# Moving VectorE's instruction-fetch jump and adding one for SyncE in a load-bound mean kernel

## The chip, the cores and the metric

The kernel runs on one core of one Trainium2 chip. The metric is the device time in microseconds (us). Smaller is better. Times of a few tenths matter here, so single runs are listed as well as medians.

Engine names: VectorE (DVE in the profile), ScalarE (ACT), TensorE (PE), GpSimd (POOL), SyncE (SP). SyncE issues all the transfers of this kernel (every DMA issue of the page stands under SPq).

## The reference

```python
x = np.random.randn(64, 256, 8192).astype(np.float32)   # 16384 rows of 32 KB, 536.87 MB
def reference(x):
    return np.mean(x, axis=2)
```

Nothing is reused: every byte is read once, summed, and 64 KB are written (the page counts 536.87 MB read and 0.07 MB written). The memory stream is the whole problem.

## The kernel before

The rows are read in 63 loads of 8 MB (128 partitions, 2 rows each), into three slots. VectorE sums each. The last 256 rows come as one row per partition and then in chunks of falling size, so that little work is left behind the last byte.

```python
    nc.vector.addr_align(FETCH_BLOCK, offset=0, max_nops=0)     # FETCH_BLOCK = 128
    ...                                                         # identity, memsets
    for n in range(LB):                                         # LB = 63
        xt = slots[n % SLOTS]                                   # SLOTS = 3
        ld = load(xt[:], x_v[n], load_sem[n % LOAD_SEMS])
        if n == 0:
            first = ld
        ...                                                     # VectorE sums xt into res
    ...                                                         # last row set: LAST_CHUNKS =
    ...                                                         #   4096, 2048, 1024, 512, 256, 256
    scaled_sum(fin[0][:, 0:1], head[:])
    store_last(0)
    untracked(scaled_sum(fin[1][:, 0:1], fin_in[:, 0 : lastw + k]))._wait_ge(sem, 16)
    store_last(1)                                               # the last store, by SyncE
    ...
    head_bb, body_bb = nc.main_func.blocks[:2]                  # head_bb ends in a barrier
    body_bb.instructions.remove(first.ins)                      # the first load goes ahead
    at = ...                                                    #   of SyncE's part of it
    head_bb.instructions.insert(at, first.ins)
```

By its name and arguments, `addr_align` asks for the engine's next instruction to stand at a multiple of `FETCH_BLOCK`, which the program calls a fetch block. What the trace of this kernel shows of it is one COMPARE_BRANCH of 47 ns on VectorE at 0.847 us. This document calls it a jump. A packet of 8192 bytes of the kind "instruction" follows at 6.616 us. This document calls it a fetch. Where an engine stands still for some tenths of a microsecond without a jump, and such a packet follows, this document reads it as the engine running on past the end of a block and calls it a "natural crossing".

## Time and profile before

| | before |
|---|---|
| device time, 3 runs | 1247.87 us (1247.67 to 1247.88) |
| span of the profiled run | 1246.0 us |
| read rate over the span | 431 GB/s |
| round (one load of 8 MB) | 19.35 us, of which VectorE sums 17.22 |

Four lines of the profile page of the kernel before: the busy tenths of the DMA engines in 40 slices of the span, then the queues with packets, bytes and share, then the chain that ended last.

```profile
DMA  9999999999999999999999999999999999999998
q1 hardware_dynamic: 10168, 536.94, 99.7%
q14 instruction: 2, 0.02, 0.0%
DMA 70%; DVE 29%; SPq 0%; issue 0%; DVEq 0%
```

The DMA engines are busy throughout (9 tenths or more in 39 of the 40 slices). The third line: two packets of 8192 bytes each, and the one at 6.616 us ran among the packets of load 0.

VectorE's timeline of the kernel before, from the start (start, duration, instruction, and in brackets how long the engine was idle before it and what ended that):

```profile
1.46 0.12 DVE L75 MEMSET fin<- 128x32 f32 x2 [1.46 <-PEq L193]
22.46 17.22 DVE L95 TENSOR_REDUCE res<-xt 128x2 f32<-128x16384 f32 x1 [20.87 <-DMA xt<-in_x_dram]
41.80 17.22 DVE L95 TENSOR_REDUCE res<-xt 128x2 f32<-128x16384 f32 x1 [2.13 <-DMA xt<-in_x_dram]
```

VectorE is ready at 1.5 us and idle for 20.87 us, until load 0 has landed. It then waits about 2.13 us in every round. The first sum starts at 22.456 us, 0.02 us after the last of load 0's sixteen semaphore events (22.433). So a short delay of VectorE's start is taken up by these 20.87 us, and a delay of a landing is taken up by nothing.

The end of the chain of waits of the kernel before (start, duration, what):

```profile
1202.25 38.48 DMA xt<-in_x_dram
1240.73 0.02 issue
1240.76 1.45 DVE fin_in L95 x3
...
1242.34 0.45 DVE fin_in L101 x2
1242.79 0.02 issue
1242.82 0.21 DVE fin_t L112
```

The chain stops at the last VectorE instruction. What follows on SyncE is seen in its own instructions of the closing lines, between 1244.6 and 1245.2 us (count, duration in ns min/median/max, first and last start):

```profile
L169 SPq DRAIN  x2: 7/60/114, 1244.7 to 1245.1; - x2
L169 SPq EVENT_SEMAPHORE  x1: 28/28/28, 1244.6 to 1244.6; - x1
```

The wait at 1244.6 is for the last store. The next wait that the trace lists for SyncE is that of the closing barrier, behind both drains, and yet the two drains stand 0.43 us apart.

### The profile page before, as it was taken

What the parts mean: (1) busy time and instruction counts of PE and PEld (TensorE: products, weight loads), DVE (VectorE), ACT (ScalarE), POOL (GpSimd) and SP (SyncE); (2) the same over time, 40 slices, a digit from 0 to 9 for tenths busy, and PEclk for the clock granted to TensorE, in tenths of its full rate; (3) what the DMA queues carried; (4) which work ended last, traced back from release to release, by engine and by line L of the source; (5) the groups of instructions that cost most, each with busy time, mean ns of one, the idle gap of its engine ahead of it and who ended that gap; (6) DMA issues with size and microseconds to landing.
All of it is one profiled execution on the core that took longest, in us unless ns stands there. A gap on an engine that the chain in (4) does not pass through costs nothing.

```text
span 1246.0 us, 224 instructions
## 1 busy us (share of the span) xinstructions
PE 0.9 (0%) x2; PEld 0.4 (0%) x2; DVE 1087.3 (87%) x79; ACT 16.4 (1%) x13; POOL 0.7 (0%) x6
## 2 busy tenths in 40 slices
PE   0000000000000000000000000000000000000000
PEld 0000000000000000000000000000000000000000
DVE  2898988989889889898898988989889889898897
ACT  0000000000000000000000000000000000000004
POOL 0000000000000000000000000000000000000000
DMA  9999999999999999999999999999999999999998
GB/s 434 425 421 438 438 438 436 438 427 417 438 438 438 438 438 436 429 414 438 438 438 438 438 436 431 412 438 438 438 438 438 436 431 417 433 438 438 438 438 339
DMA packets 10170, 536.96 MB, mean 431 GB/s; under 512 B 1145, under 2 KB 1464, under 8 KB 1720
## 3 DMA queue, kind: packets, MB, share of 16 engines
q1 hardware_dynamic: 10168, 536.94, 99.7%
q14 instruction: 2, 0.02, 0.0%
HBM read 536.87 MB, written 0.07 MB: 431 GB/s over the span
## 4 chain that ended last, share of the span: by engine, by line
DMA 70%; DVE 29%; SPq 0%; issue 0%; DVEq 0%
DMA xt<-in_x_dram 70%; DVE res L95 29%; DVE fin_in L95 0%; SPq L85 0%; DVE fin_in L101 0%; DVE fin_t L112 0%; DVEq L101 0%
## 5 line engine op out<-in xcount | busy, mean ns | idle before, releaser
L95 DVE TENSOR_REDUCE res<-xt 128x2 f32<-128x16384 f32 (+1 forms) x63 | 1076.4, 17086 | 153.1 <-DMA xt<-in_x_dram 153.1
L98 ACT ACT_TABLE_LOAD x1 | 1.3, 1283 | 1181.6 <-DVE res L95 1181.6
L98 ACT ACTIVATE xt<-xt 128x8192 f32<-128x8192 f32 (+5 forms) x6 | 14.7, 2443 | 43.9 <-DMA xt<-in_x_dram 43.7
L95 DVE TENSOR_REDUCE fin_in<-xt 128x1 f32<-128x256 f32 (+3 forms) x5 | 4.9, 1005 | 0.3 <-DMA xt<-in_x_dram 0.2
L95 DVE TENSOR_REDUCE head<-xt 128x1 f32<-128x4096 f32 x1 | 4.4, 4420 | 0.2 <-DMA xt<-in_x_dram 0.2
L156 PE MATMUL ps<-ident,res 128*63 128x128 f32 x2 | 0.9, 460 | 1230.7 <-ACT xt L98 1229.6
L75 DVE MEMSET fin<- 128x32 f32 x2 | 0.1, 85 | 1.5 <-PEq L193 1.5
L98 ACT ACTIVATION_READ_ACCUMULATOR xt<-xt 128x1 f32 x6 | 1.1, 186 | 0.0
L157 DVE TENSOR_SCALAR bulk<-ps 63x128 f32<-63x128 f32 x2 | 0.6, 278 | 0.4 <-PE ps L156 0.4
L156 PEld LDWEIGHTS ps<-ident,res 128*63 128x63 f32 x2 | 0.4, 180 | 1230.9 <-issue 1229.6
L101 DVE TENSOR_SCALAR_CACHE_REDUCE fin_in<-fin_in 128x265 f32<-128x265 f32 x1 | 0.4, 430 | 0.2 <-DVE fin_in L95 0.2
L112 DVE STREAM_TRANSPOSE fin_t<-fin 128x32 f32<-128x32 f32 x2 | 0.4, 212 | 0.1
L63 POOL TENSOR_SCALAR_AFFINE_SELECT ident<-ident 128x128 f32<-128x128 f32 x1 | 0.3, 292 | 0.1
L101 DVE TENSOR_SCALAR_CACHE_REDUCE head<-head 128x2 f32<-128x2 f32 x1 | 0.2, 155 | 0.1
L62 POOL MEMSET ident<- 128x128 f32 x1 | 0.2, 204 | 0.4 <-POOLq L193 0.4
L193 POOL MEMSET const-bfloat16-1.0<- 128x1 bf16 x1 | 0.1, 101 | 0.0
L193 POOL MEMSET const-uint8-127<- 128x1 uint8 x1 | 0.1, 101 | 0.0
L193 POOL MEMSET const-float32-0.0<- 128x1 f32 x1 | 0.1, 98 | 0.2 <-issue 0.2
L193 POOL MEMSET const-float32-1.0<- 128x1 f32 x1 | 0.1, 98 | 0.0
L101 DVE DVE_READ_ACCUMULATOR head<-head 128x1 f32 x1 | 0.1, 83 | 0.0
L101 DVE DVE_READ_ACCUMULATOR fin_in<-fin_in 128x1 f32 x1 | 0.1, 83 | 0.0
## 6 DMA issues: line engine op xcount, KB each, us to landing
xt<-in_x_dram SPq DMA_DIRECT2D x1, 4096.0 KB, 31.1
xt<-in_x_dram SPq DMA_DIRECT2D x1, 2048.0 KB, 35.7
xt<-in_x_dram SPq DMA_DIRECT2D x1, 1024.0 KB, 37.7
xt<-in_x_dram SPq DMA_DIRECT2D x63, 40.8
xt<-in_x_dram SPq DMA_DIRECT2D x1, 512.0 KB, 38.5
xt<-in_x_dram SPq DMA_DIRECT2D x1, 256.0 KB, 38.7
xt<-in_x_dram SPq DMA_DIRECT2D x1, 128.0 KB, 38.5
fin_in<-in_x_dram SPq DMA_DIRECT2D x1, 128.0 KB, 38.4
```

The source lines that it names most:

```text
L62: nc.gpsimd.memset(ident[:], 0.0)
L63: nc.gpsimd.affine_select(out=ident[:], in_=ident[:], compare_op=mybir.AluOpType.not_equal, fill=1.0, base=0, pattern=[[-1, P]], channel_m ...
L75: nc.vector.memset(fin[r][:], 0.0)
L95: return untracked(nc.vector.tensor_reduce(out=dst, in_=src, axis=X, op=ADD))
L98: return untracked(nc.scalar.activation(out=src, in_=src, func=COPY, accum_out=dst))
L101: return nc.vector.tensor_scalar(out=src, in0=src, scalar1=inv, scalar2=None, op0=mybir.AluOpType.mult, op1=ADD, accum_out=dst,)
L112: nc.vector.transpose(out=fin_t[r][:], in_=fin[r][:])
L156: nc.tensor.transpose(out=ps[:LB, :], in_=res[:, r, :], identity=ident[:])
L157: nc.vector.tensor_scalar_mul(out=bulk[:LB, :, r], in0=ps[:LB, :], scalar1=inv)
L193: nc = _bacc.Bacc("TRN2", target_bir_lowering=False, num_devices=1)
```

## The change

The intent is to keep the crossing of fetch blocks off the critical ends. VectorE's jump goes ahead of the head barrier. SyncE gets a jump while VectorE does its last sums, so that it does not cross a block after them.

```diff
-    nc.vector.addr_align(FETCH_BLOCK, offset=0, max_nops=0)
+    jump = nc.vector.addr_align(FETCH_BLOCK, offset=0, max_nops=0)
 ...
-    store_last(0)
+    st = store_last(0)
+
+    with tc.issue_after(st.ins):
+        st = nc.sync.wait_ge(tail_sem[-2], 16)
+    with tc.issue_after(st.ins):
+        st = nc.sync.addr_align(FETCH_BLOCK, offset=0, max_nops=0)
     untracked(scaled_sum(fin[1][:, 0:1], fin_in[:, 0 : lastw + k]))._wait_ge(sem, 16)
-    store_last(1)
+    with tc.issue_after(st.ins):
+        store_last(1)
 ...
-    (first.ins is moved ahead of SyncE's drain in the head)
+    for early in (first.ins, jump.ins):
+        (early is moved ahead of its own engine's drain in the head)
```

The last two entries stand for a short loop, shown in words. The first load was ahead of the barrier already.

More of the change, by code (lines that the diff above doesn't have):

```diff
@@ L112, in store_last @@
         nc.vector.transpose(out=fin_t[r][:], in_=fin[r][:])
-        nc.sync.dma_start(out=out_last[r], in_=fin_t[r][0:P:SQ, :])
+        return nc.sync.dma_start(out=out_last[r], in_=fin_t[r][0:P:SQ, :])
     for n in range(LB):
@@ L170 @@
     head_bb, body_bb = nc.main_func.blocks[:2]
-    assert first.ins in body_bb.instructions
-    body_bb.instructions.remove(first.ins)
-    at = next(
-        i
-        for i, ins in enumerate(head_bb.instructions)
-        if ins.engine == first.ins.engine and isinstance(ins, mybir.InstDrain)
-    )
-    head_bb.instructions.insert(at, first.ins)
+    for early in (first.ins, jump.ins):
+        assert early in body_bb.instructions
+        body_bb.instructions.remove(early)
+        at = next(
+            i
+            for i, ins in enumerate(head_bb.instructions)
+            if ins.engine == early.engine and isinstance(ins, mybir.InstDrain)
+        )
+        head_bb.instructions.insert(at, early)
 _INS = ['x']
```

## The prediction

> What bounds the kernel. The load stream. The page's slices show the DMA engines at least 90% busy in all slices but the last; 536.87 MB are read at 431 GB/s over a span of 1246.0 us. The chain of waits alternates loads (70%) and VectorE sums (29%), but VectorE still waits 2.1 us for a load in each round of 19.35 us, and further loads are always queued. Only the two ends can move.
>
> What the diff really does. SyncE's first load already stood ahead of the head barrier and does not move. VectorE's jump to an aligned fetch block goes ahead of the barrier; SyncE gets a wait for the last chunk but one and then a jump, ahead of its last store.
>
> Head. In the trace VectorE's branch starts at 0.85 us and its next instruction, a memset, at 1.46. That itself costs nothing, as VectorE then waits for load 0 until 22.46. What counts is a side effect. The trace's packet records show one 8192-byte instruction fetch at 6.616 us, 309 ns long, in the middle of load 0 on one DMA engine. That engine's second packet after it starts at 9.866 where the cadence of 2.418 us had it at 9.03: 0.83 us lost. This engine then lands last in load 0 (21.961 against 21.656 for the second last) and still in load 62 (0.311 us behind the second last). A load completes with its slowest engine, so the fetch costs the stream about 0.31 us. I take it to be the fetch that VectorE's jump starts, queued behind two packets. Ahead of the barrier it is asked for near 0.1 us, some 0.75 us earlier; the first load packets start from 1.04 to 1.83 (this engine's at 1.55). If it is served first, all landings come about 0.31 us earlier, and the tail follows. I give that two chances in three; otherwise nothing is gained. The barrier ends perhaps 0.1 us later, so loads 1 and 2 are issued later, which costs nothing.
>
> Tail. After the last store lands, SyncE drains at 1244.678 (7 ns); its next drain starts at 1245.113: 0.43 us, where the step before a drain takes 0.065 us at the head. Another 8192-byte fetch follows at 1245.867. I read this as SyncE running over the end of a fetch block: about 0.36 us on the critical end. [...]the packets here are 8 KiB, and the gap is not hidden. With the change the crossing falls at about 1241.6 to 1242.2, while VectorE works until 1243.03; the last store is not delayed. Gain about 0.36 us, at four chances in five.
>
> Sum: 1247.87 - 0.67 = 1247.2 if both work; weighed, 1247.3 us, range 1246.9 to 1247.8. Faster by over 2%: 0.005; within 2%: 0.99; slower by over 2%: 0.005.
>
> Right if: the early fetch lies before about 1.5 us, the last of load 0's sixteen landings is near 21.65, rounds stay 19.35, SyncE's gap between those drains is about 0.07 us, its branch stands near 1241.6 and the late fetch near 1242.5.
>
> Wrong if: the early fetch still falls among the load's packets, or another engine caused it; the 0.43 us gap is a drain's or branch's own cost and stays; the jump puts code after the kernel onto another block end, outside the span; or runs on a chip differ by more than these tenths.

The sum stands: 1247.87 less 0.67 us (0.31 at the head, 0.36 in the tail) is 1247.2 us if both work. That a load completes with its slowest engine is seen in the trace: the second last of load 0's sixteen semaphore events is at 21.996 us and the last at 22.433, and the first sum starts 0.02 us after the last.

## The result and the profile after

| | before | changed |
|---|---|---|
| device time | 1247.8 us median of 6 (1247.67 to 1248.61) | 1247.2 us median of 6 (1247.08 to 1247.47) |
| span of the profiled run | 1246.0 us | 1245.3 us |

The ratio is 0.9995, with a 95% interval of 0.9982 to 1.0008. A ratio is computed as the mean time of one kernel's runs over that of the other's, so it is not quite the ratio of the medians. This interval is wider than every difference. What is said below of tenths rests on the lists of single runs and on stretches of the traces that repeat from run to run.

VectorE's timeline of the changed kernel at the start:

```profile
1.03 0.13 DVE L75 MEMSET fin<- 128x32 f32 x2 [1.03 <-PEq L200]
22.46 17.22 DVE L95 TENSOR_REDUCE res<-xt 128x2 f32<-128x16384 f32 x1 [21.30 <-DMA xt<-in_x_dram]
41.81 17.22 DVE L95 TENSOR_REDUCE res<-xt 128x2 f32<-128x16384 f32 x1 [2.12 <-DMA xt<-in_x_dram]
```

The memsets come 0.43 us earlier and load 0 not at all: the first sum starts at 22.46 as before. At the start nothing was gained.

The end of the chain of waits of the changed kernel:

```profile
1202.07 38.49 DMA xt<-in_x_dram
1240.56 0.02 issue
1240.59 1.42 DVE fin_in L95 x3
...
1242.15 0.45 DVE fin_in L101 x2
1242.60 0.02 issue
1242.62 0.21 DVE fin_t L112
```

This is 0.2 us earlier than before, although load 0 was not. Comparing the starts of all 63 sums, the kernel before lost 0.11 us in one round (19.46 us in place of 19.35) that the changed kernel did not lose. Experiment 2 comes back to it.

SyncE's drains of the changed kernel between 1244.45 and 1244.65 us, and then the two instructions that the change added:

```profile
L175 SPq DRAIN  x2: 7/10/13, 1244.5 to 1244.6; - x2
```

```profile
L166 SPq NOP  x1: 14/14/14, 1241.6 to 1241.6; - x1
L166 SPq COMPARE_BRANCH  x1: 33/33/33, 1241.6 to 1241.6; - x1
```

The drains stand 0.07 us apart in place of 0.43, and the second takes 7 ns in place of 114. The jump stands at 1241.6 us, while VectorE still works until 1242.83. The trace's record of SyncE's wait for the last store starts only when the store has landed (1244.608 us with its last semaphore event at 1244.591 before, 1244.421 with 1244.405 after). From there to the start of SyncE's last instruction it is 1244.608 to 1245.904 before (1.296 us) and 1244.421 to 1245.240 after (0.819 us), a gain of 0.477 us. It is the gap of 0.37 us plus 0.107 us of the longer drain.

The fetches of the changed kernel lie at 4.195 and 1242.952 us in the trace's packet records (6.616 and 1245.867 before). The DMA view of the changed kernel from 4.18 to 4.52 us shows the first among the packets of the load:

```profile
q1 hardware_dynamic: 9, 0.59, 410.0%
q14 instruction: 1, 0.01, 5.7%
```

So the fetch came earlier but not early enough: the load's packets were already running, the first since 1.041 us.

### The profile page after: what moved, and what is told of

Its sections match the earlier page's. It is cut to its first block, busy times and chain, and to the rows that moved or that the text cites. A ratio compares the mean times of both kernels' runs of the same rounds, so it can differ in the third digit from the quotient of the medians.

```text
span 1245.3 us, 226 instructions
## 1 busy us (share of the span) xinstructions
PE 0.9 (0%) x2; PEld 0.4 (0%) x2; DVE 1087.3 (87%) x79; ACT 16.4 (1%) x13; POOL 0.7 (0%) x6
## 4 chain that ended last, share of the span: by engine, by line
DMA 70%; DVE 29%; SPq 0%; issue 0%; DVEq 0%
DMA xt<-in_x_dram 70%; DVE res L95 29%; DVE fin_in L95 0%; SPq L85 0%; DVE fin_in L101 0%; DVE fin_t L112 0%; DVEq L101 0%
```

## The experiments

After this result there were two theories. Theory A: the whole lasting gain is SyncE's block crossing, about 0.47 us, and VectorE's earlier jump gives nothing because its fetch still falls among load packets. Theory B: VectorE's earlier jump also made the stream 0.15 to 0.2 us shorter, as the earlier chain above suggests.

Kernels 1 to 4 ran on one chip with shared runs of the kernel before (9 runs, 1247.54 to 1247.95, median 1247.73). So did 5 to 8 (1247.65 to 1248.35, median 1247.82) and 9 to 11 (1247.58 to 1248.23, median 1247.83). Each kernel had 5 runs, and all gave correct results. The changed kernel itself ran in the first result and with kernels 1 to 4, where it was 0.6 and 0.48 us below the kernel before. Differences between groups cross chips; for them the distance to the kernel before is given too.

The columns from the third on are of the profiled run: the first fetch after the start, the last of load 0's sixteen landings in the packet records, and the closing stretch on SyncE as above, from the end of its wait for the last store to its last instruction.

| kernel | median (range), us | first fetch | load 0 landed | closing stretch |
|---|---|---|---|---|
| before | see above | 6.616 | 21.961 | 1.296 |
| changed, first run | 1247.2 (1247.08 to 1247.47) | 4.195 | 21.963 | 0.819 |
| 1 changed again | 1247.25 (1247.10 to 1247.49) | 4.178 | 21.943 | 0.819 |
| 2 head move alone | 1247.84 (1247.50 to 1248.31) | 4.556 | 22.320 | 1.297 |
| 3 SyncE's jump alone | 1247.22 (1247.17 to 1247.36) | 6.906 | 22.246 | 0.819 |
| 4 no VectorE jump | 1247.41 (1247.22 to 1248.05) | 838.857 | 21.751 | 0.814 |
| 5 SyncE's jump, no wait | 1247.32 (1247.07 to 1247.46) | 4.281 | 22.053 | 0.813 |
| 6 second VectorE jump | 1248.20 (1248.06 to 1248.38) | 4.393 and 588.147 | 22.158 | 0.819 |
| 7 load behind barrier | 1247.71 (1247.58 to 1247.84) | 1.246 | 22.491 | 0.813 |
| 8 jump behind last store | 1247.17 (1246.97 to 1247.32) | 4.316 | 22.086 | 0.818 |
| 9 VectorE jump first of all | 1247.32 (1247.10 to 1247.54) | 4.423 | 22.185 | 0.820 |
| 10 load behind SyncE's drain | 1247.42 (1247.19 to 1247.51) | 4.186 | 21.952 | 0.813 |
| 11 kernels 8 and 9 together | 1247.45 (1247.12 to 1247.80) | 4.305 | 22.074 | 0.818 |

### 1. The changed kernel again

No edit.

> The changed kernel once more, for the same-chip comparison. Both theories: 0.5 to 0.65 us below the kernel before. Theory A (all of the lasting gain is SyncE's block crossing, 0.36 us of gap plus 0.11 us of drain; the 0.19 us by which the load stream ended earlier in the first profile is scatter of the stream): the span difference averages about 0.47 us. Theory B (VectorE's earlier jump also made the stream 0.15 to 0.2 us shorter): about 0.65 us. The early fetch packet is expected among load 0's packets, near 4.2 us, again.

It was 0.48 us below the kernel before by the medians, and the two lists of runs do not overlap (its slowest is 1247.49, the fastest run of before 1247.54). That is theory A's number.

### 2. The head move alone

```diff
-    with tc.issue_after(st.ins):
-        st = nc.sync.wait_ge(tail_sem[-2], 16)
-    with tc.issue_after(st.ins):
-        st = nc.sync.addr_align(FETCH_BLOCK, offset=0, max_nops=0)
```

> Only VectorE's jump moves; SyncE keeps its natural crossing. Theory A: within 0.1 us of the kernel before; fetch packet near 4.2 us, one engine still 0.84 us behind its cadence, load 0 lands at about 21.96. Theory B: 0.15 to 0.2 us below the kernel before. In both SyncE's gap between its two drains after the last store is 0.43 us again.

It was 0.11 us above the kernel before by the medians, and the lists overlap. Theory B wanted it 0.15 to 0.2 us below. SyncE's two drains of this kernel, between 1245.2 and 1245.75 us:

```profile
L171 SPq DRAIN  x2: 7/60/114, 1245.2 to 1245.7; - x2
```

The gap is back, and so is the drain of 114 ns. The profiled run lost time in two rounds of the stream (19.465 and 19.673 us in place of 19.35), which the kernel before also did, in a different round and by less. Kernels 7, 10 and 11 show such rounds too (up to 19.517, 19.411 and 19.498), and kernels 1, 3, 5, 8 and 9 none above 19.38. So the 0.11 us by which the first profile of before ran late lies inside what the stream scatters. What makes such a round was not found.

### 3. SyncE's jump alone

```diff
-    for early in (first.ins, jump.ins):
+    for early in (first.ins,):
```

> Only SyncE's wait and jump; VectorE's jump stays behind the barrier. Theory A: 0.4 to 0.5 us below the kernel before, equal to the changed kernel within 0.1 us; fetch packet near 6.6 us. Theory B: 0.4 to 0.5 us below before, but 0.15 to 0.2 us above the changed kernel.

It was 0.51 us below before and within 0.03 us of the changed kernel on the same chip, with its fetch at 6.906 us. SyncE's two drains of this kernel, between 1244.7 and 1244.9 us, stand as in the changed kernel:

```profile
L175 SPq DRAIN  x2: 7/10/13, 1244.8 to 1244.8; - x2
```

Together with experiment 2 this settles where the gain came from: SyncE's jump gives all of it, and VectorE's move gives nothing that can be seen.

### 4. No VectorE jump at all

```diff
-    jump = nc.vector.addr_align(FETCH_BLOCK, offset=0, max_nops=0)
-    for early in (first.ins, jump.ins):
+    for early in (first.ins,):
```

> SyncE's jump kept, VectorE's jump taken out[...]. If the 8192-byte fetch near 4.2 us is the one that VectorE's jump starts, it is gone from there, load 0 lands with its second slowest engine at about 21.5 to 21.7 instead of 21.96, and a fetch appears later, 1.3 us or more after a gap of about 0.5 us between two VectorE instructions. If that gap falls in a wait for a load the time is about that of the changed kernel (a late fetch still delays the same engine by 0.8 us); if it falls among the last sums, about 0.5 us is lost there and up to 0.3 us gained from the stream. If another engine causes the fetch, the packet near 4.2 us stays.

The 0.8 us is the estimate from the 0.83 us lost in the trace of before. That a late fetch runs on the same engine is not shown here or in kernel 6, as the packet records carry no engine number.

The fetch among load 0's packets is gone, so it is the one that VectorE's jump starts. Load 0 landed at 21.751 us (21.5 to 21.7 was expected); the eight runs with the early jump, the load at 0 us and a fetch among the packets landed at 22.10 on average (the mean of their rows in the table: changed, 1, 2, 5, 6, 8, 9, 11; from 21.943 to 22.320). The DMA view of this kernel from 0 to 23 us has only one queue left, and the one from 838.8 to 839.2 us shows where the fetch went:

```profile
q1 hardware_dynamic: 160, 9.44, 97.3%
```

```profile
q1 hardware_dynamic: 3, 0.20, 123.7%
q14 instruction: 1, 0.01, 5.2%
```

VectorE's timeline around it:

```profile
834.86 17.22 DVE L94 TENSOR_REDUCE res<-xt 128x2 f32<-128x16384 f32 x1 [2.13 <-DMA xt<-in_x_dram]
854.84 17.22 DVE L94 TENSOR_REDUCE res<-xt 128x2 f32<-128x16384 f32 x1 [2.76 <-DMA xt<-in_x_dram]
```

The fetch ran at 838.857 us, inside the sum that lasts from 834.86 to 852.08. If it followed its crossing, as the fetches of the other traces follow their jumps by 1.02 to 6.1 us, VectorE's natural crossing was over before the wait for the load began at 852.08, and cost VectorE no time that the trace shows. Its fetch does cost: the load in flight lands late, and that round takes 19.98 us in place of 19.35. The gain at the start is paid back in round 42, and the time is that of the changed kernel within the scatter. So the jump at the head does not avoid the cost of the fetch (0.63 us in round 42 here). It moves it.

### 5. SyncE's jump without its wait

```diff
-    with tc.issue_after(st.ins):
-        st = nc.sync.wait_ge(tail_sem[-2], 16)
```

> The changed kernel without SyncE's wait for the last chunk but one: the jump follows the first small store at once, near 1237.6 us, and its 8192-byte fetch is asked for near 1238.9, while the small chunks still come in. If a fetch delays its DMA engine whenever loads are queued on it, the fetch lands among the packets of the chunks and the last landings are 0 to 0.8 us later, by as much as that engine was not ahead of the slowest; the crossing itself is still hidden. Time equal to the changed kernel up to 0.5 us above it. Rival: the fetch costs nothing so late, and the wait is idle care: equal to the changed kernel within 0.1 us.

The jump stood at 1237.725 us and its fetch ran at 1240.935, among the last chunks, 3.2 us after it. The time is within 0.12 us of the changed kernel's (1247.2 and 1247.25 in its two sets) and 0.15 us above kernel 8, with overlapping lists. By the distance to the kernel before (0.50 us, against 0.48 and 0.6 for the changed kernel) it is no slower either. The trace says the same: the last chunk landed 1.315 us after the last chunk but three, against 1.312 in the changed kernel (semaphore events). This does not tell a small cost from none, but no gain from the wait can be seen.

### 6. A second VectorE jump in the middle

```diff
+        if n == 30:
+            with tc.issue_after(prev.ins):
+                prev = nc.vector.addr_align(FETCH_BLOCK, offset=0, max_nops=0)
 ...
```

(`prev` is VectorE's last instruction; each sum is queued behind it, to hold the place of the jump.)

> The changed kernel with one more VectorE jump ahead of sum 30, in a wait of 2.1 us for a load. Theory: the jump of about 0.57 us is hidden in that wait, but it starts one more 8192-byte fetch on the same DMA engine, which is late already, so that engine loses another 0.84 us and every later landing with it: 0.7 to 0.85 us above the changed kernel, one round of about 20.2 us instead of 19.35. Rival: the stream absorbs a single fetch over the remaining rounds: equal to the changed kernel within 0.2 us.

VectorE's timeline around it:

```profile
583.82 17.22 DVE L95 TENSOR_REDUCE res<-xt 128x2 f32<-128x16384 f32 x1 [2.12 <-DMA xt<-in_x_dram]
604.12 17.22 DVE L95 TENSOR_REDUCE res<-xt 128x2 f32<-128x16384 f32 x1 [3.08 <-DMA xt<-in_x_dram]
```

The jump itself:

```profile
L122 DVEq COMPARE_BRANCH  x1: 47/47/47, 583.8 to 583.8; - x1
```

The jump stood at 583.834 us, so it was hidden behind sum 29, which had just started, and not in the wait for load 30 as the expectation had it. That round took 20.30 us in place of 19.35, so one more fetch cost 0.955 us, and the following 32 rounds gave none of it back: every landing after it was late by as much. On the same chip the device time is 0.88 us above kernel 5 (1248.20 against 1247.32) and 0.38 above the kernel before; against the changed kernel on the other chip it is 0.95 (1247.25). Its list of runs overlaps with neither of those two; with that of before it does. The rival falls. The expectation (0.7 to 0.85) was a little low. In the packet records the fetch itself, at 588.147, takes 332 ns, and the packet that starts as it ends takes 3080 ns where 2418 is usual: together 0.99 us on that engine, about the 0.955 that the stream lost.

### 7. The first load behind the barrier

```diff
-    for early in (first.ins, jump.ins):
+    for early in (jump.ins,):
```

> The changed kernel, but the first load goes behind the head barrier, so that VectorE's jump is 0.8 to 0.9 us ahead of it. If what makes the fetch costly is that load packets are queued before it, it is now served first, at about 1.3 to 1.4 us; no packet of load 0 is held for 0.84 us, the slowest engine ends within 0.6 us of the median, and load 0 lands 19.7 to 20.2 us after its first packet, against 20.9 in the changed kernel. The load itself starts some 0.5 to 0.9 us later in the span (SyncE reaches the barrier sooner), so the whole comes out between 0.3 us faster and 0.5 us slower. Rival: the 0.84 us is spent anyway: 0.5 to 0.9 us slower than the changed kernel.

Now the fetch was served first, at 1.246 us, 1.14 us after the jump at 0.102. The DMA view of this kernel from 1.2 to 1.9 us has no packet of a load yet:

```profile
q14 instruction: 1, 0.01, 4.9%
```

Load 0's sixteen landings then lay within 0.53 us, with no single engine left behind; in the changed kernel they spread over 0.97 us with the slowest 0.42 us behind the second slowest. SyncE issued the load 0.95 us later than in the changed kernel, and load 0 landed only 0.39 us later than the average of 22.10. The cost of the fetch is real and can be avoided, but holding the load back costs more than it saves: 1247.71 us, which is only 0.11 us below the kernel before on the same chip, 0.39 above kernel 5 there, and 0.46 above the changed kernel on the other chip. The expected time from first packet to landing was missed (20.51 us measured, 19.7 to 20.2 expected).

### 8. SyncE's jump behind the last store

```diff
-    with tc.issue_after(st.ins):
-        st = nc.sync.wait_ge(tail_sem[-2], 16)
-    with tc.issue_after(st.ins):
-        st = nc.sync.addr_align(FETCH_BLOCK, offset=0, max_nops=0)
     ...
     with tc.issue_after(st.ins):
-        store_last(1)
+        st = store_last(1)
+    with tc.issue_after(st.ins):
+        nc.sync.addr_align(FETCH_BLOCK, offset=0, max_nops=0)
```

> SyncE's jump behind the last store, with no wait before it: the crossing falls between the issue of the store (ends near 1243.37) and its landing (near 1244.2). If only a crossing on the critical end costs, this is as fast as the changed kernel within 0.1 us, with the jump taking about 0.5 us inside that wait and a gap of about 0.07 us between the two drains. If the crossing costs wherever it stands after the last sums, or delays the store's descriptors, it is 0.2 to 0.5 us slower than the changed kernel.

SyncE's jump and then its closing waits and drains in this kernel:

```profile
L167 SPq COMPARE_BRANCH  x1: 33/33/33, 1243.5 to 1243.5; - x1
```

```profile
L173 SPq EVENT_SEMAPHORE  x3: 28/28/28, 1244.0 to 1244.5; - x3
L173 SPq DRAIN  x2: 7/7/7, 1244.6 to 1244.6; - x2
```

After the jump at 1243.514 the next instruction starts at 1243.977, so the jump takes 0.46 us in all. It takes them out of the wait for the store's landing, which SyncE leaves at 1244.514. The closing stretch is 0.818 us and the time 1247.17, 0.65 us below the kernel before of its chip: as good as the changed kernel, with one wait less. So it is not that a crossing is expensive as such (the jump of 0.46 us leaves a closing stretch of 0.818 us here, against 1.296 before): before, it stood a few instructions too late, behind that wait instead of ahead of it.

### 9 to 11. Three tries at getting the fetch ahead of load 0

Kernel 9 puts VectorE's jump ahead of its register set-up:

```diff
-            if ins.engine == early.engine and isinstance(ins, mybir.InstDrain)
+            if ins.engine == early.engine
+            and (early is jump.ins or isinstance(ins, mybir.InstDrain))
```

> The changed kernel with VectorE's jump moved further ahead, to the very first instruction of the program on VectorE, ahead of its register set-up. In the runs so far a fetch follows its jump by 1.15 to 1.3 us and the load packets start at 1.0 to 2.0 us, so the jump at 0.1 us is only just too late. If the jump now stands some tenths of a microsecond before the span's start, its fetch runs before 1.0 us, ahead of load 0: no engine is held for 0.84 us, load 0 lands near 21.75 as without any VectorE jump (21.9 to 22.3 in the runs with the fetch among its packets), and the time is 0.2 to 0.4 us below the changed kernel. Rival: the set-up takes no time, the jump stays near 0.1 us, the fetch stays among the packets and the time is that of the changed kernel.

Kernel 10 lets SyncE's drain go first:

```diff
-        head_bb.instructions.insert(at, early)
+        head_bb.instructions.insert(at + (early is first.ins), early)
```

> The changed kernel with SyncE's first load behind SyncE's own drain, still ahead of the barrier's wait: load 0 is held back by about 0.07 us. If that is enough to let the fetch through on its engine (it missed the engine's first packet by about 0.1 us in the changed kernel's profile, as far as its request can be placed), the fetch appears before 2 us and 0.2 to 0.4 us are gained, less 0.07; if not, the time is that of the changed kernel plus 0 to 0.1 us.

Kernel 11 has kernel 9's edit and kernel 8's.

> VectorE's jump first of all, with SyncE's jump behind the last store in place of the one with the wait: the two variants that promise most, together. If VectorE's early fetch gets ahead of load 0, about 0.3 us below the changed kernel, near 1246.9; if not, equal to it.

The rivals were right in each. In kernels 9 and 11 the jump stayed at 0.094 and 0.093 us, so going ahead of the set-up won no time that the trace shows. In kernel 10 the load began 0.085 us later, which was not enough. In all three the fetch ran after its engine's first packet (4.423, 4.186 and 4.305 us), and none beat the changed kernel: they are 0.51, 0.41 and 0.38 us below the kernel before of their chip. Of all eleven none does clearly; kernel 8 equals it with one wait less.

## Why the prediction was right or wrong

The predicted time was 1247.3 us, with a range of 1246.9 to 1247.8; measured were 1247.2 and, in a second set, 1247.25. That the number fits is in part luck. Weighed by its own odds, the prediction held about 0.21 us for the head (0.31 at two in three) and 0.29 for the tail (0.36 at four in five); the head brought nothing and the tail 0.477, so two errors nearly cancelled.

**The stream bounds the kernel, and only the ends move: right.** Rounds stayed at 19.35 us in every kernel, apart from the slow ones named above.

**"If it is served first, all landings come about 0.31 us earlier": the cost was about right, and it did not happen.** The fetch at 6.616 us is VectorE's (experiment 4: no jump, no fetch there). It costs about what was estimated: load 0 landed 0.35 us earlier without it, in one run against an average of eight that scatter by 0.38. How much of an engine's delay the load feels differs from run to run: in these eight the slowest landing was between 0.05 and 0.89 us behind the second slowest. The 0.955 us of experiment 6 is nearly the whole delay of the engine, as would be so if that engine was already among the last; the records, which carry no engine number, do not show whether it was. The cost comes in two parts. These are the packet records of the engine that ran the fetch, in the kernel before (start and duration in ns), put together by matching ends to starts (to within 4 ns):

```
start    took   what
 4202    2418   64 KB of load 0
 6616     309   8 KB of instructions
 6922    2948   64 KB of load 0
 9866    2418   64 KB of load 0
```

The fetch takes 0.309 us, and the packet after it 0.53 us more than its neighbours (2.948 us against 2.418). In mid-stream it was 0.332 and 0.66 us (kernel 6). The fetch on q14 stands between two packets of q1. Its turn did not come at once: by the estimate below, this fetch was asked for at 1.9 to 2.2 us (the jump at 0.847 plus 1.02 to 1.32), and yet one more packet of the load went ahead of it at 4.202. In kernel 6 too, one more started at 585.732, after the time near 585 at which its fetch was asked for by the same estimate. Why is open. By this matching the engine that fetched lands last in load 0 (21.961 us in the packet records, the second last at 21.656), and the first sum starts 0.02 us after the last semaphore event of the load; hence the whole load waited for the one that fetched.

**"Ahead of the barrier it is asked for near 0.1 us ... two chances in three": this is the step that failed.** The jump did move from 0.847 to 0.094 us. Its fetch did not run ahead of the load, in any of the eight profiled runs with this jump and the load in its early place. The mis-sized term is the time from a jump to its fetch. The prediction took it as nothing. Where no load is queued ahead, it is 1.14 us (kernel 7, at the start) and, for SyncE's jump at the end, 1.02 to 1.32 us in ten traces (kernel 1, 1241.650 to 1242.667; changed kernel, 1241.632 to 1242.952). Behind load packets it is 3.2 to 6.1 us (SyncE in kernel 5, VectorE in kernel 3). The engine itself runs on before that: its next instruction came 0.46 us after the jump on SyncE (1243.514 to 1243.977, kernel 8) and 0.57 us on VectorE (0.094 to 0.666, changed kernel), in both cases before the fetch had run. So the request arrives about 1.1 to 1.4 us into the span, an estimate from these, and the load's first packets start between 1.04 and 2.06 (changed kernel). In these eight traces and in kernel 10's, the packet just ahead of the fetch had started at 1.131 to 1.224 us (1.176 in the changed kernel), so far as the matching of records tells; the fetch of kernel 7, with no load before it, started at 1.246. The early fetch missed its place by little. The fetch then waited for one packet in place of two and cost as much as before (the packet after it took 2.954 us, and load 0 landed at 21.963 against 21.961). The prediction had placed its engine's packet at 1.55 us, from a single trace of the kernel before, and no trace with the early jump has it so late.

**"Gain about 0.36 us, at four chances in five": right, and undersized.** The gap, read as SyncE's natural crossing, stood between the two drains behind its wait for the last store, and the gain was 0.477 us: 0.37 us of gap, as predicted, and 0.107 us because the drain after the gap took 114 ns in place of 7. The closing stretch repeats to 0.007 us: 1.296 and 1.297 us in the two traces without SyncE's jump, 0.813 to 0.820 us in the eleven with it. It was not hidden, as it stood behind the last wait (kernel 8 hides its jump of 0.46 us ahead of that wait).

**"The late fetch near 1242.5": wrong**, at 1242.95 (1242.67 in kernel 1), by the same mis-sized time from jump to fetch.

**Loads 1 and 2 later by 0.1 us: right, and free.** SyncE issued load 1 at 0.951 in place of 0.825 us, and the first sum started at 22.46 us in both.

What stays open: the first profile of the changed kernel had its last sums 0.19 us earlier than the profile of before. Experiments 2 and 3 do not show this as an effect of the change, and 0.11 us of it is one slow round of before. The rest was not traced.

## What to carry to other kernels

In this kernel a fetch of 8 KB among the packets of a saturated load stream held a load back: by 0.35 us at the start (kernel 4, one run against the average of eight), by 0.63 us in round 42 (kernel 4) and by 0.955 us in round 29 (kernel 6). So count the fetches that fall into the stream and look at where the slowest landing comes from. Idle time of the engine that jumps did not hide this: the second jump of kernel 6 stood hidden behind a sum, and its fetch ran 4.3 us later (583.834 to 588.147) among the packets of a load. SyncE's own crossing, on the other hand, was free once it stood in a wait that existed anyway, the one between the last store and its landing (kernel 8: the jump took 0.46 us, and the closing stretch was 0.818 us in place of 1.296). So shift it out of the few instructions behind such a wait.
